# Convolution taps as diagonal products on TensorE, and products straight from PSUM, in a gated delta mixer

## The chip, the cores and the metric

The kernel runs on one core of a Trainium2 chip. The metric is the device time of one execution in microseconds; what is compared is the median of several runs. The core has five engines with a queue each: TensorE (PE) multiplies, VectorE (DVE) and ScalarE (ACT) work elementwise, GpSimd (POOL) too, and SyncE (SP) issues the transfers. All work is ordered by semaphores that the program sets.

## The reference, cut to what matters

Two transformer blocks follow each other; the second has four parts: a mixer "ab", an MLP, a mixer "c" and another MLP. The mixer "ab" projects 272 tokens (16 of them meta tokens) by one weight, and one half of it is a bidirectional gated delta rule with 4 heads of 128 channels. What concerns this case of it:

```python
def centred_conv(x, w):                      # k = 5 taps
    y = xp[:, 0:n] * w[0]
    for j in range(1, k):
        y = y + xp[:, j:j + n] * w[j]
    return y

def gated_delta_chunked(q, k, v, beta, g):   # one direction
    kb = k * beta[..., None]
    a_mat = jnp.where(strict, jnp.einsum('bhnid,bhnjd->bhnij', kb, k) * decay, 0.0)
    rhs = jnp.concatenate([v * beta[..., None], kb * jnp.exp(gc)[..., None]], axis=-1)
    sol = lax.linalg.triangular_solve(a_mat, rhs, left_side=True, lower=True, unit_diagonal=True)
    ...
    def step(s, xs):
        v_new = u_n - jnp.einsum('bhck,bhkv->bhcv', w_n, s)
        o = jnp.einsum('bhck,bhkv->bhcv', q_n, s) + jnp.einsum('bhij,bhjv->bhiv', qk_n, v_new)
        s = s * gl_n[..., None, None] + jnp.einsum('bhck,bhcv->bhkv', k_n, v_new)
        return s, o

def delta_mixer(hq, hk, hv, hz, hb, ha, conv_w, a_log, dt_bias, o_gain):
    qkv = jax.nn.silu(centred_conv(jnp.concatenate([hq, hk, hv], axis=-1), conv_w))
    ...
    fwd = gated_delta_chunked(q, k, v, beta[:, :, 0], g[:, :, 0])
    bwd = rev(gated_delta_chunked(rev(q), rev(k), rev(v), rev(beta[:, :, 1]), rev(g[:, :, 1])))
```

So v is a projection, then a convolution with five taps per channel, then silu; and its rows are multiplied by a step size beta per token and head, another one for each direction.

## The kernel before

The 272 tokens lie in the free dimension, channels in the partitions: a block of v is 128 channels x 272 tokens, and v has four, numbered 8 to 11 among the blocks of the projection. Chunks are three pieces of tokens, t = 0 (16 rows) and t = 1, 2 (128 rows); the forward direction goes through them as 0, 1, 2 and the backward one as 2, 1, 0.

The work of `delta` is written as Python generators which yield after each small step, and whose steps are put into one program order: `spread(gen, fill, share)` runs, after each step of `gen`, so many steps of `fill`. The main line is `side` (norms and decay matrices) and then `levels`, which inverts the triangular matrices for both directions: `blocks` inverts blocks of 32 x 32 in four levels, each with two `product`s (L1700) and, on VectorE, a subtraction (L1714) and a transpose (L1716), and `pairs` joins them to blocks of 128 in four steps (products L1739, L1746 and L1749, L1756, L1761). After it `scan` runs three steps for both directions in turn: L1830 multiplies the inverse by v times beta, L1842 gives the new state, L1857 the output. The fill is `filling`: first the late projection blocks 19, 20 and 12 to 15 (`rest`), then the windowed attention of the other half of the mixer (products L1545 and L1568, softmax on L1511 to L1516), and after each of its steps 1.4 steps (`VS`) of `values`. This `values` makes v: `rest` projects the blocks 8 to 11 (each is three fp32r products, high and low parts, L272 to L274, for each of 8 pieces of the inner dimension, issued in groups of six) and convolves each in `conv_late`; `silu_exp` follows (Exp, minimum on L241, Ln and Exp, and a GpSimd product on L1359); then `turned` turns v's channels into rows by transposes on TensorE (L297) and copies them out of PSUM on ScalarE (L1622). In the rows and the order, `xp` goes by the name `dec`, the helper lines L241 and L245 stand for every scale and multiply-add, and L267 for the split of a weight into high and low part. What `values` has left when the levels end runs ahead of the scan.

In `conv_late` VectorE multiplies the projected block by the norm's scale (L1366), puts it into a padded tile `xp`, and applies the five taps: one scale (`ts`, L241) and four multiply-adds (`stt`, L245). In the scan `pmul` (L1594) multiplies v's turned rows by beta on GpSimd into a tile `vb`, once for each direction and piece, and the same function makes `kdn`, k times a decay, from which L1842 makes the state.

`self.slot(hold="delta")` takes one of a few 1 MB places of SBUF for the length of the mixer; `self.ring` brings a block of weights into the next free one, and the transfer is issued on SyncE. PSUM tiles come from two rotating sets, `bank` and `aux`. `bank` is a full PSUM bank for the products, `aux` one for small steps.

Of the kernel before, what the change touches and what calls it, by code (L numbers as in the profile page):

```python
# [25 lines left out]
N2 = S + 16  # L26
# [154 lines left out]
class Kern:  # L181
# [1178 lines left out]

    def conv_late(self, p, b, rs, wc, y):
        nc = self.nc
        xp = p.tile([128, 512], F32, name="dec", bufs=3)
        nc.gpsimd.memset(xp[:, 0:2], 0.0)
        nc.gpsimd.memset(xp[:, N2 + 2:N2 + 4], 0.0)
        nc.vector.tensor_mul(xp[:, 2:N2 + 2], b, rs)  # L1366
        self.ts(y, xp[:, 0:N2], wc[:, 0:1])
        for j in range(1, 5):
            self.stt(y, xp[:, j:j + N2], wc[:, j:j + 1], y, OP.mult, OP.add)

    def ab_inproj(self, c1, p1, px, full, steps):
# [63 lines left out]
        self.exp_set(last)  # L1435

        def rest(pw, some, bank=self.bank):
            for i in some:
                b = bank()[:, :N2]
                hi, lo = self.wsplit(blk(i), nc.gpsimd if i in WP else None)  # L1440
                for k in range(8):
                    c = slice(k * 128, (k + 1) * 128)
                    self.mm3(b, (hi[:, c], lo[:, c]), (u[0][:, k], u[1][:, k]), k == 0, k == 7)
                    if k % 2 and k < 7:
                        yield
                if i >= 12:
                    nc.vector.tensor_mul(z[:, i - 12] if i < 16 else qw[:, i - 16], b, rs)
                else:
                    self.conv_late(pw, b, rs, cw[:, i], v[:, i - 8])
                yield  # L1450
# [125 lines left out]
    def delta(self, c1, p1, pw, qk, v, z, qw, vba, rest, norms, qw_norms):  # L1576
        nc, a = self.nc, self.a
        mm = nc.tensor.matmul
        def new(tag, bufs, n=128):
            if n < 128:  # L1580
                return pw.tile([128, 4 * n], F32, name=tag + "s", bufs=2)
            return pw.tile([128, 512], F32, name=tag, bufs=bufs)
# [10 lines left out]
        def pmul(out, x, y_):  # L1593
            nc.gpsimd.tensor_mul(out, x, y_)  # L1594
# [5 lines left out]

        two = [self.slot(hold="delta") for _ in range(2)]
        kn, vn = (t[:, :1536].rearrange("p (t c) -> p t c", t=3) for t in two)

        tc_ = [t[:, 1536:1824] for t in two]
        slot = self.slot(hold="delta")
        ac, uc = ([slot[:, i * 576 + d * 288:i * 576 + (d + 1) * 288] for d in range(2)] for i in range(2))

# [4 lines left out]
        for d in range(2):  # L1612
            nc.gpsimd.memset(ac[d][:, 256:288], 0.0)

        def turned(dst, x):
# [162 lines left out]
        def values():  # L1778
            yield from rest(pw, [8, 9, 10, 11])
            for h in range(4):  # L1780
                self.silu_exp(pw, v[:, h], v[:, h])
                yield
            yield from turned(vn, v)

# [22 lines left out]
        def scan(step, d):  # L1807
# [7 lines left out]
            s0 = st[d]  # L1815
            vb = new("dec", 3)
            pmul(v4(vb)[:n], v4(vn[:, t])[:n], bc(beta[:n, t, hs], n, 128))
            if step:
# [9 lines left out]
            for h in range(4):  # L1828
                o = slice(h * 128, (h + 1) * 128)
                mm(b[:n, o], u[h], vb[:n, o], start=True, stop=step == 0)  # L1830
                if step:
                    mm(b[:n, o], wT[:, h * n:(h + 1) * n], st[d][:, o], start=False, stop=True)
# [404 lines left out]
def layouts(inp):  # L2237
# [68 lines left out]
    fa = np.concatenate([fa, np.zeros((128, 3 * 1024), np.float32)], 1)  # L2306
    o["w_ab"] = ca(fa.reshape(128, 6, 4096).transpose(1, 0, 2))
    o["w_vba"] = ca(form_b(wab[:, np.concatenate([2704 + r(128), 2048 + r(16)])]))
    prm["conv_w"] = f["conv_w_a_2"][0].T.reshape(12, 128, 5).transpose(1, 0, 2).reshape(128, 60)
# [53 lines left out]
```

## Time and profile before

| | us |
|---|---|
| median of 3 runs (lowest, highest) | 1550.58 (1544.03, 1555.73) |
| the profiled execution | 1552.06 |
| its span on the core | 1550.3 |
| TensorE busy | 1480.6 (96%) |
| VectorE busy | 820.3 (53%) |
| ScalarE busy | 638.5 (41%) |
| GpSimd busy | 175.9 (11%) |

The profiled execution's mean granted TensorE clock is 0.971 of full speed; the two levels seen are 1.2 GHz (0.5) and 2.4 GHz (1.0), and a value between is a mean of both over a stretch. Times in the rows further down are counted from the start of the span. The mixer's late projections, inverse and scan lie between about 905 and 1050 us. Engine work overlaps, so a busy share is no price: what counts is which wait ends last.

### The profile page before, as it was taken

To read this page: it belongs to the slowest core of one execution; us is meant where nothing else is said; L and a number is where in the kernel's file an instruction comes from. 1 tells how busy PE (TensorE), PEld (TensorE's weight loads), DVE (VectorE), ACT (ScalarE), POOL (GpSimd) and SP (SyncE) were. 2 spreads that over 40 slices of the span, in tenths; PEclk is the share of its full clock that TensorE was granted. 3 is DMA by queue.
4 is the path that set the end of the run, shared out by engine and by line. 5 is a ranking of instruction groups with operands and counts; after the bars stand their busy time and mean duration, and the time that the engine had idled before them with its cause. 6 is when DMAs were issued, how large, how long until landed. Compare 5 with 4: busy or idle time off the path is not lost.

```text
span 1550.3 us, 26421 instructions
## 1 busy us (share of the span) xinstructions
PE 1480.6 (96%) x10806; PEld 1130.8 (73%) x10806; DVE 820.3 (53%) x1594; ACT 638.5 (41%) x1265; POOL 175.9 (11%) x226
## 2 busy tenths in 40 slices
PE   8999999989899999999998888899999999999999
PEld 7788744344388875434338877679999997899998
DVE  6686712212436782222128586557556666666665
ACT  5475411111246642111127664455444455554443
POOL 0130000000001000000005440302001123121000
PEclk9999999999999999999999898799999999999999
DMA  9345799999833579999953300036555542255530
GB/s 377 128 136 213 303 402 421 386 421 422 351 147 110 209 307 378 421 377 422 422 233 121 120 29 4 26 125 231 180 174 171 185 144 92 82 197 182 181 138 29
DMA packets 50033, 348.76 MB, mean 225 GB/s; under 512 B 5616, under 2 KB 6896, under 8 KB 8688
## 3 DMA queue, kind: packets, MB, share of 16 engines
q1 hardware_dynamic: 49904, 346.97, 58.2%
q8 instruction: 89, 1.46, 0.4%
q14 instruction: 40, 0.33, 0.1%
HBM read 345.90 MB, written 1.05 MB: 224 GB/s over the span
## 4 chain that ended last, share of the span: by engine, by line
PE 43%; DVE 4%; POOL 3%; ACT 2%; issue 2%; POOLq 0%; ACTq 0%; DVEq 0%
PE bank L274 10%; PE bank L272 10%; PE bank L273 10%; PE bank L1060 3%; PE bank L1101 2%; POOL cy L1346 1%; PE aux L297 1%; PE aux L2072 1%; ACT ring L236 1%; PE aux L1568 1%; DVE ring L267 1%; PE bank L1700 1%; PE aux L2050 1%; PE bank L1857 1%; PE aux L1545 0%
## 5 line engine op out<-in xcount | busy, mean ns | idle before, releaser
L236 ACT ACTIVATE ring<-ring 128x1024 fp32r<-128x1024 f32 (+3 forms) x189 | 186.9, 999 | 202.2 <-PE bank L274 180.2
L267 DVE TENSOR_TENSOR ring<-ring,ring 128x1024 fp32r<-128x1024 f32 x145 | 179.3, 1236 | 88.5 <-ACT ring L236 88.5
L272 PE MATMUL bank<-uh,ring 128*128 128x272 f32 (+1 forms) x744 | 219.3, 295 | 0.0
L274 PE MATMUL bank<-uh,ring 128*128 128x272 f32 (+1 forms) x744 | 215.6, 290 | 0.0
L273 PE MATMUL bank<-ul,ring 128*128 128x272 f32 (+1 forms) x744 | 214.5, 288 | 0.0
L272 PEld LDWEIGHTS bank<-uh,ring 128*128 128x128 f32 x744 | 141.7, 190 | 3.3 <-issue 2.2
L274 PEld LDWEIGHTS bank<-uh,ring 128*128 128x128 f32 x744 | 141.7, 190 | 0.8 <-DVE ring L267 0.4
L273 PEld LDWEIGHTS bank<-ul,ring 128*128 128x128 f32 x744 | 141.6, 190 | 0.7
L274 PE MATMUL bank<-rh,ring 128*128 128x272 f32 (+1 forms) x496 | 141.6, 286 | 0.0
L272 PE MATMUL bank<-rh,ring 128*128 128x272 f32 (+1 forms) x496 | 141.5, 285 | 0.0
L273 PE MATMUL bank<-rl,ring 128*128 128x272 f32 (+1 forms) x496 | 140.9, 284 | 0.0
L1073 DVE TENSOR_TENSOR hid<-hid,bank 128x512 f32<-128x512 f32 x16 | 11.0, 687 | 193.3 <-PE bank L1060 193.3
L273 PEld LDWEIGHTS bank<-rl,ring 128*128 128x128 f32 x496 | 93.8, 189 | 0.0
L272 PEld LDWEIGHTS bank<-rh,ring 128*128 128x128 f32 x496 | 93.2, 188 | 0.0
L274 PEld LDWEIGHTS bank<-rh,ring 128*128 128x128 f32 x496 | 93.0, 187 | 0.0
L245 DVE SCALAR_TENSOR_TENSOR big<-bank,gs,big 128x512 fp32r<-128x512 f32 x32 | 24.0, 751 | 99.3 <-ACT big L236 97.8
L1309 POOL TENSOR_TENSOR fr<-fr 128x272 f32<-128x272 f32 (+1 forms) x64 | 40.1, 627 | 287.7 <-DVE fr L245 283.8
L236 ACT ACTIVATE big<-bank,gs 128x512 fp32r<-128x512 f32 x32 | 22.0, 687 | 98.4 <-PE bank L1101 98.2
L1279 DVE TENSOR_TENSOR h<-h,bank 128x272 f32<-128x272 f32 (+1 forms) x80 | 33.2, 426 | 50.8 <-PE bank L274 50.8
L236 ACT ACTIVATE hid<-bank 128x512 f32<-128x512 f32 x24 | 14.3, 597 | 108.9 <-PE bank L1060 103.9
L1083 ACT COPY hidT<-bank 128x512 f32<-128x512 f32 x16 | 9.4, 586 | 118.3 <-PE bank L297 118.3
L1101 PE MATMUL bank<-big,hidT 128*64 128x512 f32 x208 | 47.8, 595 | 0.1
(677 smaller groups left out, 3434.3 us busy)
## 6 DMA issues: line engine op xcount, KB each, us to landing
ring<-w_ff SPq DMA_DIRECT2D x58, 1024.0 KB, 4.8
big<-w_gate SPq DMA_DIRECT2D x30, 1024.0 KB, 17.7
big<-w_up SPq DMA_DIRECT2D x29, 1024.0 KB, 18.0
big<-w_down SPq DMA_DIRECT2D x26, 1024.0 KB, 17.6
ring<-w_gate SPq DMA_DIRECT2D x24, 1024.0 KB, 14.2
ring<-w_down SPq DMA_DIRECT2D x24, 1024.0 KB, 17.5
ring<-w_up SPq DMA_DIRECT2D x20, 1024.0 KB, 18.6
big<-w_in SPq DMA_DIRECT2D x9, 1024.0 KB, 11.2
```

The costliest lines, as they stand in the source:

```text
L236: return self.nc.scalar.activation(out, in_, func, **kw)
L245: return (eng or self.nc.vector).scalar_tensor_tensor(out, in0, s, in1, op0=op0, op1=op1, **kw)
L267: (eng or self.nc.vector).tensor_sub(l, src, h.bitcast(F32))
L272: mm(out, lhs[0], rhs[0], start=first, stop=False)
L273: mm(out, lhs[0], rhs[1], start=False, stop=False)
L274: mm(out, lhs[1], rhs[0], start=False, stop=last)
L297: self.nc.tensor.transpose(out, in_, self.ident[:k, :k])
L1060: mm(b[e * 64:e * 64 + CAP], xg[:, k, e * CAP:(e + 1) * CAP], w[:, (2 * k + e) * 512:(2 * k + e + 1) * 512], start=k == 0, stop=k == 7)
L1101: mm(yb[n][e * 64:e * 64 + CAP], hT[:, k, e * 64:e * 64 + CAP], w[:, o:o + 512], start=k == 0, stop=k == 3)
L1279: self.nc.vector.tensor_add(self.h2[:, k, lo:], self.h2[:, k, lo:], b[:, :n])
L1309: nc.gpsimd.tensor_mul(r, r, r)
L1346: nc.gpsimd.tensor_add(y, y, t)
```

## The change

`conv_late` becomes a generator. After the multiplication into `xp` it yields, and four of the five taps are then products on TensorE that add up in one `aux` tile: each has a 128 x 128 diagonal matrix of the tap's weights as one operand and a shifted view of `xp` as the other. The fifth tap and the sum are one multiply-add on VectorE. The sixteen diagonal matrices (four blocks, four taps) come as a new input `w_dg` of 1 MB, loaded into a slot held for the mixer when `rest` first runs.

`turned` is no longer used for v. In `turned_v` the transposes of a piece go to a PSUM tile, and VectorE multiplies that tile by beta for both directions into `VB`; the forward direction at t = 0 has its four heads in one tile, the backward one has three there and the fourth in `last`. In the scan `vb` is taken from `VB`, and the GpSimd product is gone. The pieces come in the order 0, 2, 1. `VB` needs places, so the slots that weight blocks and other tiles get are others than before.

```diff
-    def conv_late(self, p, b, rs, wc, y):
+    def conv_late(self, p, b, rs, wc, y, turns):
         nc.vector.tensor_mul(xp[:, 2:N2 + 2], b, rs)
-        self.ts(y, xp[:, 0:N2], wc[:, 0:1])
-        for j in range(1, 5):
-            self.stt(y, xp[:, j:j + N2], wc[:, j:j + 1], y, OP.mult, OP.add)
+        yield
+        cb = self.aux()[:, :N2]
+        for i, j in enumerate((0, 1, 3, 4)):
+            nc.tensor.matmul(cb, turns[:, i * 128:(i + 1) * 128], xp[:, j:j + N2], start=i == 0, stop=i == 3)
+        self.stt(y, xp[:, 2:2 + N2], wc[:, 2:3], cb, OP.mult, OP.add)
...
         def rest(pw, some, bank=self.bank):
+            if not diag:
+                diag.append(self.slot(hold="delta"))
+                nc.sync.dma_start(diag[0], a["w_dg"])
...
-                    self.conv_late(pw, b, rs, cw[:, i], v[:, i - 8])
+                    yield from self.conv_late(pw, b, rs, cw[:, i], v[:, i - 8], diag[0][:, (i - 8) * 512:(i - 7) * 512])
...
-        two = [self.slot(hold="delta") for _ in range(2)]
-        kn, vn = (t[:, :1536].rearrange("p (t c) -> p t c", t=3) for t in two)
+        one, two = (self.slot(hold="delta") for _ in range(2))
+        kn = one[:, :1536].rearrange("p (t c) -> p t c", t=3)
...
+        VB = {(d, t): two[:, (2 * d + t - 1) * 512:(2 * d + t) * 512] for d in range(2) for t in (1, 2)}
+        VB[0, 0], VB[1, 0] = slot[:, 1440:1952], pw.tile([16, 384], F32, name="vb0", bufs=1)
+        last = one[:, 1824:1952]
...
+        def turned_v():
+            for t in (0, 2, 1):
+                cc = self.hcols(t)
+                n = cc.stop - cc.start
+                b = self.bank()
+                for h in range(4):
+                    self.transpose(b[:n, h * 128:(h + 1) * 128], v[:, h, cc])
+                for d in range(2):
+                    m = 4 if d == 0 or t else 3
+                    nc.vector.tensor_mul(VB[d, t][:n].rearrange("p (h c) -> p h c", h=m), v4(b)[:n, :m],
+                                         beta[:n, t, 4 * d:4 * d + m, None].to_broadcast([n, m, 128]))
+                    if m == 3:
+                        self.ts(last[:n], b[:n, 384:512], beta[:n, t, 7:8])
+                yield
...
-            yield from turned(vn, v)
+            yield from turned_v()
...
-            vb = new("dec", 3)
-            pmul(v4(vb)[:n], v4(vn[:, t])[:n], bc(beta[:n, t, hs], n, 128))
+            vb = VB[d, t]
+            vh = [last if d and t == 0 and h == 3 else vb[:, h * 128:(h + 1) * 128] for h in range(4)]
...
-                mm(b[:n, o], u[h], vb[:n, o], start=True, stop=step == 0)
+                mm(b[:n, o], u[h], vh[h][:n], start=True, stop=step == 0)
...
+    for i in range(4):
+        for k, j in enumerate((0, 1, 3, 4)):
+            dg[r(128), i, k, r(128)] = f["conv_w_a_2"][0][j, 1024 + i * 128:1152 + i * 128]
+    o["w_dg"] = dg.reshape(128, 2048)
```

How this stands in the queues is shown at three places. First TensorE, at the first product of the second level, where `ring,am` is the last piece of that level's first product, L297 with `ws` are transposes of the window's softmax and L272 to L274 are a block of the projection (six to a step, of which the first and the last are shown). Before:

```order
L1700 MATMUL bank<-ring_6932,am 32x32 x35
L272 MATMUL bank<-uh,ring_7771 128x272
L273 MATMUL bank<-ul,ring_7771 128x272
...
L274 MATMUL bank<-uh,ring_7771 128x272
L297 MATMUL aux<-prm,ws 16x128
L297 MATMUL aux<-prm,ws 128x128 x2
L272 MATMUL bank<-uh,ring_7771 128x272
...
L274 MATMUL bank<-uh,ring_7771 128x272
L1700 MATMUL bank<-qk,ring_6933 32x32 x72
```

and with the change, with its lines moved by 26:

```order
L1726 MATMUL bank<-ring_6933,am 32x32 x32
L1371 MATMUL aux<-dec,two_6952 128x272 x4
L297 MATMUL aux<-prm,ws 16x128
L297 MATMUL aux<-prm,ws 128x128 x2
L272 MATMUL bank<-uh,ring_7782 128x272
...
L274 MATMUL bank<-uh,ring_7782 128x272
L1726 MATMUL bank<-qk,ring_6933 32x32 x72
```

Block 8's four products (L1371) stand there in front of one group of six, where two groups stood.

The second place is TensorE in the pairs, from the first product (L1739, now L1765) to the last (L1761, now L1787). Before:

```order
L274 MATMUL bank<-uh,ring_8240 128x272
L1739 MATMUL bank<-wsp_6931,ring_6938 32x32 x16
L1739 MATMUL bank<-ring_6932,ring_6942 32x32 x16
...
L272 MATMUL bank<-uh,ring_8240 128x272
...
L1568 MATMUL aux<-PTw,vba 64x128 x6
L1746 MATMUL bank<-qk,ring_6938 32x32 x8
...
L297 MATMUL aux<-prm,ws 128x128 x2
L1756 MATMUL bank<-T,ring_6938 64x64 x8
L1756 MATMUL bank<-T,ring_6942 64x64 x8
L1568 MATMUL aux<-PTw,vba 64x128 x6
...
L1761 MATMUL bank<-ring_6938,qk 64x64 x8
L1761 MATMUL bank<-ring_6942,qk 64x64 x8
```

with the change:

```order
L1765 MATMUL bank<-ring_6933,ring_6943 32x32 x10
L1371 MATMUL aux<-dec,two_6952 128x272 x4
L1765 MATMUL bank<-ring_6933,ring_6943 32x32 x6
...
L272 MATMUL bank<-uh,ring_8394 128x272
...
L1576 MATMUL aux<-PTw,vba 64x128 x6
...
L1775 MATMUL bank<-ring_6943,qk 32x32 x16
L272 MATMUL bank<-uh,ring_8394 128x272
...
L1782 MATMUL bank<-T,ring_6943 64x64 x8
L272 MATMUL bank<-uh,ring_8394 128x272
...
L1576 MATMUL aux<-PTm,vba 64x16 x6
L1371 MATMUL aux<-dec,two_6952 128x272 x4
L1787 MATMUL bank<-ring_6939,qk 64x64 x8
```

Block 10's four products stand inside the first product, block 11's ahead of the last one; and block 11's projection products (two groups of six behind L1775, one behind L1782) stand where before the last of them (the row above L1739 is the end of the last group) were done.

The third place is GpSimd, from v's silu (L1359 with `v`) through the scan, `T` and `am` being `kdn`. Before:

```order
L1359 TENSOR_TENSOR v<-v,dsq 128x272 x2
L1594 TENSOR_TENSOR T<-wsp_6931,dt_6918 128x512 x3
L1359 TENSOR_TENSOR v<-v,dsq 128x272 x2
L1594 TENSOR_TENSOR dec<-ring_6932,dt_6893 16x512
L1594 TENSOR_TENSOR dec<-ring_6932,dt_6893 128x512 x3
L1359 TENSOR_TENSOR z<-z,dsq 128x272
L1594 TENSOR_TENSOR dec<-ring_6932,dt_6893 128x512
L1594 TENSOR_TENSOR am<-wsp_6931,dt_6918 16x512
L1359 TENSOR_TENSOR z<-z,dsq 128x272 x3
L1594 TENSOR_TENSOR dec<-ring_6932,dt_6893 16x512
```

with the change:

```order
L1359 TENSOR_TENSOR v<-v,dsq 128x272 x3
L1602 TENSOR_TENSOR T<-wsp_6931,dt_6918 128x512 x3
L1359 TENSOR_TENSOR v<-v,dsq 128x272
L1359 TENSOR_TENSOR z<-z,dsq 128x272
L1602 TENSOR_TENSOR am<-wsp_6931,dt_6918 16x512
L1359 TENSOR_TENSOR z<-z,dsq 128x272 x3
```

The six products into `dec` (L1594, one direction and piece each) have gone from between v's and z's; `am` is now behind one product of z.

## Rows read from the trace of the kernel before

**Rows 1.** The page: busy time by engine, and GB/s in 40 slices.
```profile
PE 1480.6 (96%) x10806; PEld 1130.8 (73%) x10806; DVE 820.3 (53%) x1594; ACT 638.5 (41%) x1265; POOL 175.9 (11%) x226
...
GB/s 377 128 136 213 303 402 421 386 421 422 351 147 110 209 307 378 421 377 422 422 233 121 120 29 4 26 125 231 180 174 171 185 144 92 82 197 182 181 138 29
```

**Rows 2.** Busy times by stretch, 920 to 1025; columns in the first row.
```profile
core 0: us, PE busy (x) PEld busy (x) DVE busy (x) ACT busy (x) POOL busy (x), PEclk, DMA share, GB/s
...
920.00:960.00 40.00, 33.37 (x1269) 27.15 (x1268) 25.70 (x78) 16.52 (x53) 6.35 (x10) 0.81 0.02 4
960.00:972.00 12.00, 12.00 (x285) 10.58 (x285) 11.46 (x31) 7.51 (x22) 3.70 (x3) 1.00 0.02 5
972.00:980.00 8.00, 4.29 (x24) 2.27 (x24) 7.17 (x16) 5.55 (x16) 4.40 (x5) 0.76 0.00 0
980.00:1000.00 20.00, 18.06 (x97) 14.59 (x96) 9.85 (x24) 9.89 (x30) 6.41 (x8) 0.58 0.00 1
1000.00:1025.00 25.00, 23.93 (x203) 20.31 (x201) 11.97 (x32) 10.64 (x29) 1.03 (x1) 1.00 0.55 191
```

**Rows 3.** Chain of waits, 965 to 987: start us, us, what.
```profile
965.92 0.44 DVE dec L1366
...
971.38 0.41 DVE v L245
...
974.34 0.77 POOL v L1359
...
975.56 1.48 ACT ring L1622 x3
...
984.84 1.04 POOL dec L1594
985.88 1.06 POOL am L1594
...
986.98 4.08 PE bank L1842 x16
```

**Rows 4.** TensorE's waits, 905 to 1050: in total, times, longest us.
```profile
PE bank L1830 <- POOL dec L1594: 2.5, 1, 2.5
...
PE bank L1842 <- POOL am L1594: 1.6, 1, 1.6
```

**Rows 5.** Chain of waits, 878 to 888, fp32 products (L1407) and one projection product.
```profile
878.71 1.81 PE aux L1407 x4
...
887.20 0.46 PE aux L1407 x2
887.66 0.12 PE bank L272
```

**Rows 6.** VectorE by line and form: duration ns min/median/max, first and last start.
```profile
L1676 DVE TENSOR_TENSOR ring<-aux,dec x4: 669/678/691, 895.4 to 909.1; 128x512 f32<-128x512 f32 x4
...
L1820 DVE TENSOR_TENSOR ring<-wsp,dt x3: 679/680/684, 971.7 to 976.4; 128x512 f32<-128x512 f32 x3
L1820 DVE TENSOR_TENSOR am<-wsp,dt x1: 670/670/670, 1013.4 to 1013.4; 16x512 f32<-16x512 f32 x1
...
L241 DVE TENSOR_SCALAR v<-dec,wsp x4: 340/358/361, 913.1 to 966.6; 128x272 f32<-128x272 f32 x4
...
L245 DVE SCALAR_TENSOR_TENSOR v<-dec,wsp,v x16: 480/496/979, 914.2 to 971.3; 128x272 f32<-128x272 f32 x16
```

**Rows 7.** Timeline of TensorE, 961 to 979: start, us, what [idle before].
```profile
961.25 0.60 PE L1739 MATMUL bank<-wsp,ring 32*32 32x32 f32 x26
...
970.04 1.90 PE L1761 MATMUL bank<-ring,qk 64*64 64x64 f32 x32
...
978.20 1.88 PE L1830 MATMUL bank<-dec,us 16*16 16x128 f32 x8 [2.51 <-POOL dec L1594]
```

**Rows 8.** Chain of waits, later: a product and a late split.
```profile
1004.49 1.83 PE bank L1842 x16
...
1040.48 1.15 DVE ring L267
```

More of the change, by code (lines that the diff above doesn't have):

```diff
@@ L1435, in ab_inproj @@
         self.exp_set(last)
+        diag = []
         def rest(pw, some, bank=self.bank):
+            if not diag:
+                diag.append(self.slot(hold="delta"))
+                nc.sync.dma_start(diag[0], a["w_dg"])
             for i in some:
@@ L1599, in delta @@
         beta, gc, gl, ec, kd, kb = self.gates(c1, p1, vba)
-        two = [self.slot(hold="delta") for _ in range(2)]
-        kn, vn = (t[:, :1536].rearrange("p (t c) -> p t c", t=3) for t in two)
-        tc_ = [t[:, 1536:1824] for t in two]
+        one, two = (self.slot(hold="delta") for _ in range(2))
+        kn = one[:, :1536].rearrange("p (t c) -> p t c", t=3)
         slot = self.slot(hold="delta")
+        tc_ = [one[:, 1536:1824], slot[:, 1152:1440]]
+        VB = {(d, t): two[:, (2 * d + t - 1) * 512:(2 * d + t) * 512] for d in range(2) for t in (1, 2)}
+        VB[0, 0], VB[1, 0] = slot[:, 1440:1952], pw.tile([16, 384], F32, name="vb0", bufs=1)
+        last = one[:, 1824:1952]
         ac, uc = ([slot[:, i * 576 + d * 288:i * 576 + (d + 1) * 288] for d in range(2)] for i in range(2))
@@ L2307, in layouts @@
     o["w_ab"] = ca(fa.reshape(128, 6, 4096).transpose(1, 0, 2))
+    dg = np.zeros((128, 4, 4, 128), np.float32)
+    for i in range(4):
+        for k, j in enumerate((0, 1, 3, 4)):
+            dg[r(128), i, k, r(128)] = f["conv_w_a_2"][0][j, 1024 + i * 128:1152 + i * 128]
+    o["w_dg"] = dg.reshape(128, 2048)
     o["w_vba"] = ca(form_b(wab[:, np.concatenate([2704 + r(128), 2048 + r(16)])]))
```

## The prediction, made before the changed kernel ran

> **What bounds the kernel now.** I read the page's busy shares first: TensorE is busy 96% of the span [rows 1]. The change lies in the delta mixer of the second block, so I then took the busy times by stretch [rows 2]. TensorE has little cover to spare there, in three different ways. From 960 to 972 us it is busy 12.00 of 12 us at a granted clock of 1.00 (the 2.4 GHz level), with VectorE busy 11.46: there the pairs of the triangular inverse are solved and v's last block is convolved. From 972 to 980 it is busy 4.29 of 8 us at a mean clock of 0.76. From 980 to 1000 it is busy 18.06 of 20 us, but at 0.58, close to the 1.2 GHz level. So one place is full, the next is starved, and the third is full of slow work. Over the 105 us of those rows TensorE is idle for 13; what is added to it has to find those holes.
>
> The chain of waits says what starves it [rows 3]. Block 11 of v is convolved on VectorE from 965.92 to 971.79, silu's last GpSimd product starts at 974.34, three ScalarE copies bring the turned rows out of PSUM (1.48 us), and later, in the scan, a GpSimd product of v by the step sizes (1.04 us) stands in front of another GpSimd product (1.06 us) for which TensorE waits until 986.98. TensorE's own waits agree: 2.5 us for the first of these products, 1.6 us for the one queued behind it [rows 4].
>
> **Part 1, the convolutions.** Four blocks lose one scale and three of four multiply-adds each on VectorE, 0.36 + 3 x 0.50 = 1.9 us at the median of the multiply-adds [rows 6], 7.4 us in all. Sixteen fp32 products of 128 x 128 by 272 columns come to TensorE. That shape is in the trace under another line [rows 5]. The row marked x2 is one product, since each fp32 product leaves two records: 0.46 us at the full clock. The row marked x4 is two at the half clock, 0.91 each. Sixteen cost 7.4 us at the full clock and 14.5 at the half. So what VectorE saves is what TensorE pays, and TensorE is the busier engine.
>
> *Blocks 8 and 9* meet the levels of the inverse. Block 8's four products stand behind the first product of the second level, where six projection products stood (0.12 to 0.13 us each at the full clock [rows 5]); block 9's stand behind a second product, and again six projection products fewer stand there. From 920 to 960 TensorE is idle 6.6 of 40 us [rows 2], because in each level it waits for VectorE's subtraction and transposes, and only a product that falls into such a wait is free. Bounds: 0 (all eight inside the idle time) and +5 (none hidden, half of them at the half clock: 4 x 0.46 + 4 x 0.91 = 5.5, less the projection products that give way). I take +1.2, nearer to the lower end: the idle time is as long as the eight products, and VectorE has 1.9 us less per block to do ahead of its transposes.
>
> *Blocks 10 and 11* meet the pairs. Before, the first product of the pairs starts at 961.25, the last at 970.04 with 1.90 us [rows 7], so the stage takes 10.7 us and TensorE is never idle in it. In the order, block 10's four products now stand inside the pairs' first product and block 11's ahead of the last: 8 x 0.46 = +3.7 us on the path. The extra step that a convolution now takes also shifts the order: 18 projection products of block 11 leave the place ahead of the pairs and stand behind their second and third products, 18 x 0.125 = +2.3 us. Where they stood they partly filled the levels' waits, so of their leaving I count only the six right before the pairs as given back, -0.8.
>
> *From the last pair to the scan* 6.3 us pass now (971.94 to 978.20 [rows 7]). The copies on ScalarE and a GpSimd product leave this stretch, 1.48 + 1.04 [rows 3], and one VectorE product out of PSUM enters it. Against that, block 11's silu starts later relative to TensorE, and VectorE's queue holds two 64-row scalings of the pairs and a softmax step in front of silu's minimum. Between 4.5 us (only the legs count) and 8.5 (only the queue counts) I take 6.5, +0.2.
>
> **Part 2, v's rows.** Gone are three ScalarE copies, 1.48 us together, and six GpSimd products of about 1.04, 6.2 us [rows 3]. VectorE gets six multiplications from PSUM into SBUF and one scale of 16 rows. Nearest rows: a product of a PSUM tile by an SBUF tile, 128 x 512, 0.68 us; one from SBUF alone, 0.68; one from SBUF with 16 rows, 0.67 [rows 6]. So 6 x 0.68 + 0.3 = 4.4 us. Only the first of these stands in front of the scan, and it is in the 6.5 above; VectorE is busy 9.85 of 20 us from 980 to 1000 [rows 2], which hides the others. By the Trainium skill (VectorE: DVE Perf Modes, Rules for kernel authors) elementwise work on a matmul's output should either take PSUM's slower reading or copy first "if you'll do many ops", which speaks against two products per tile straight from PSUM. The rows just named show no such price at this width, so the rule would add a copy of some 0.5 us per tile and save nothing.
>
> In the scan GpSimd then has nothing in front of the product for which TensorE waited: -1.6 [rows 4]. If another chain is late there instead, this is 0.
>
> **Part 3, what follows.** By the same shift one pair of window heads comes ahead of the scan, into the stretch from 972 to 980 where TensorE idles, instead of into the scan: about 2.5 us of work less at the slow clock, -2.5, or 0 if the start waits for it. Toward the end of the mixer a late split [rows 8] now comes early, but two splits for the next stage stand between the last norms on VectorE: +1, between -1 and +3 (a split is 1.15 us).
>
> **Part 4, the diagonals.** 1 MB more passes SyncE's queue, ahead of the last four weight blocks: at the 422 GB/s of the fullest slices [rows 1], 2.5 us of transfer. The DMA engines are at 2% from 920 to 972 [rows 2]. What is queued behind it are the weight blocks, which are split and multiplied only after other blocks. So 0, and at most +2.5 if one of them is needed just as it lands.
>
> **The sum.** Up to the scan: 1.2 + 3.7 + 2.3 - 0.8 + 0.2 = +6.6. Scan: -1.6 - 2.5. Tail +1, diagonals 0. Together **+2.5**. The bounds, from the low and the high end of every term, are -3 and +16; not all high ends can come at once, for the idle time that one leaves takes up another's, so I use +12. The profiled execution took 1552.06 us (span 1550.3), 1.5 above the median 1550.58, and the result is a median: 1550.6 + 2.5 = **1553**.
>
> **Rivals.** *The clock stays up.* In the stretch from 972 to 980 TensorE is half idle, and the clock after it is low [rows 2]; sixteen records of one product of the scan cost 4.08 us there and 1.83 later [rows 3, 8]. With more TensorE work up to 978 and shorter legs, the low clock could start later or not at all. The 18 us of work from 980 to 1000 would shrink by up to 9; of that the scan's own chains let about two thirds through, -6 to -9 beside the sum: 1546. For it: two legs leave the idle stretch. Against it: silu's chain of five dependent steps stays. The Trainium skill (TensorE: Matmul & The Clock Gate, Part 1) holds that the slow clock is the default and activity lifts it; by that rule this rival gains, and the rows from 960 to 1000 agree as far as they go.
>
> *The products are free.* If the 13 us of idle time take all that is added, the legs alone count: -1.5 - 1.0 - 1.6 = -4, 1546.5. Against it: the pairs' 12.00 of 12.
>
> *The slow clock spreads over the scan.* This one ends slower. If v's last block comes later than everything else, its products closing the pairs and its multiply-add standing behind other work on VectorE, TensorE idles ahead of the scan for longer than the 2.51 us of now [rows 7], and the low clock reaches past 1000: the 23.93 us of work from 1000 to 1025 [rows 2] would take up to twice as long. At 0.5 for half of it, +12, with the 6.6 of the later start +18: 1569. It decides once the way from the last pair to the scan exceeds the 8.5 us of the upper bound above.
>
> **How the numbers follow.** The sum as forecast (1550 to 1559): 0.55. The clock stays up: 0.17. The products free: 0.16. The slow clock spreads: 0.08. The rest, 0.04, to either side. The range leaves 2 in 10 out at most: from 1542 (the clock rival with its -9 and 0.3% for the runs' scatter, of which 1544 is the lowest) to 1563 (the sum with +12). About 1%, 15.5 us, is what a measurement of this kernel can tell from no change. To be faster by that needs both gains and more, 0.05; slower needs the third rival, 0.07; between them 0.88.
>
> **What would show it.** The four products of a block at 0.46 us each in the pairs and up to 0.91 in the levels; the last pair 6 to 7 us later; no wait of TensorE for GpSimd at the scan's first product or at the state's; the clock by stretch from 975 to 1025. The prediction is wrong if the scan starts less than 3 or more than 10 us later, or if the low clock after it ends elsewhere than at 1000 plus that shift.

## The result, and the profile after

The changed kernel takes 1562.1 us (median of 14 runs, 1554.3 to 1568.7) against 1549.2 us before (14 runs): a ratio of 1.0077, with a 95% interval of 1.0057 to 1.0096, so it is some 12 us slower. The sign and the range of the prediction hold, the range by less than 1 us at its upper end of 1563; its +2.5 is too small by almost 10.

The busy times of the changed kernel by stretch, with the columns of [rows 2]:

```profile
core 0: us, PE busy (x) PEld busy (x) DVE busy (x) ACT busy (x) POOL busy (x), PEclk, DMA share, GB/s
920.00:960.00 40.00, 34.36 (x1188) 27.90 (x1178) 19.98 (x72) 16.19 (x54) 4.88 (x8) 0.78 0.09 30
960.00:972.00 12.00, 11.91 (x215) 9.77 (x214) 7.55 (x20) 6.61 (x18) 0.76 (x1) 0.86 0.01 3
972.00:980.00 8.00, 7.45 (x95) 6.19 (x94) 6.31 (x7) 3.43 (x7) 4.44 (x3) 1.00 0.01 3
980.00:1000.00 20.00, 16.46 (x97) 11.17 (x96) 13.69 (x42) 10.25 (x35) 4.41 (x5) 0.74 0.00 1
1000.00:1025.00 25.00, 23.93 (x184) 19.04 (x183) 8.97 (x29) 9.46 (x28) 0.76 (x1) 0.89 0.37 125
```

Against [rows 2], VectorE is busy 7.55 us where it was busy 11.46, from 960 to 972. Part of that is relief and part is work that comes later, for from 980 to 1000 it is busy 13.69 where it was 9.85. And TensorE's clock from 960 to 972 is 0.86 instead of 1.00, the starved stretch has moved behind 980, and the slow clock with it. The 0.89 from 1000 to 1025, where it was 1.00, isn't the end of that slow stretch but a second one, as steps of 5 us show:

```profile
985.00:990.00 5.00, 4.16 (x18) 2.04 (x18) 3.88 (x14) 3.72 (x14) 2.48 (x3) 0.52 0.00 0
990.00:995.00 5.00, 4.69 (x23) 3.30 (x23) 2.92 (x9) 1.50 (x4) 0.00 (x0) 0.50 0.02 3
995.00:1000.00 5.00, 5.00 (x37) 4.06 (x35) 2.45 (x5) 2.90 (x10) 1.93 (x2) 0.95 0.00 0
...
1020.00:1025.00 5.00, 5.00 (x21) 1.91 (x19) 0.00 (x0) 0.59 (x1) 0.00 (x0) 0.50 0.59 203
```

From 1000 to 1015 the clock is 1.00; the second slow stretch lasts, with a faster part between 1030 and 1035 (0.80), until 1045.

The timeline of TensorE shows the four groups of diagonal products (two records each), the last product of the pairs and the scan's first (start, us, what, idle before):

```profile
929.46 4.00 PE L1371 MATMUL aux<-dec,two 128*128 128x272 f32 x8
...
947.87 2.10 PE L1371 MATMUL aux<-dec,two 128*128 128x272 f32 x8
...
961.73 3.58 PE L1371 MATMUL aux<-dec,two 128*128 128x272 f32 x8
...
976.48 2.07 PE L1371 MATMUL aux<-dec,two 128*128 128x272 f32 x8 [0.55 <-DVE dec L1367]
978.48 1.90 PE L1787 MATMUL bank<-ring,qk 64*64 64x64 f32 x32
...
988.32 1.88 PE L1856 MATMUL bank<-ring,us 16*16 16x128 f32 x8 [0.73 <-DVE ring L1635]
```

Against [rows 7], the last product of the pairs starts 8.4 us later and the scan 10.1 us later. Two groups ran mostly at the half clock (about 0.9 to 1.0 us a product), two mostly at the full one (about 0.5): 11.75 us in all, between the 7.4 and 14.5 of the prediction.

To compare stages between executions, I count from the first start of the decay matrices' products (L1664 before, L1690 after), for the stages ahead of it, which the change doesn't touch, scatter by some 7 us (that start lies between 885.1 and 892.1 in the profiles below). The stages end with the first starts of the levels' products, of the pairs' first, with the last start of the pairs' last, with the first starts of the scan's L1830 and of the last norms (L1871), and with the next part's first GpSimd sum (L1255). In us, worked out from first and last starts by line:

```
             to levels  levels  pairs  gap   scan  tail  rest    all
before            27.9    41.3   10.4   6.5  51.7  22.8  497.6  658.2
after             27.5    44.3   19.8   8.1  51.0  22.4  497.1  670.2
```

The 12.0 us of the two profiles agree with the 12.9 of the medians. The pairs take 9.4 us more, the levels 3.0, the gap between the last pair and the scan 1.6, and the scan gives back only 0.7. Counted from the common start, the scan begins 13.6 us later.

The chain of waits of the changed kernel through the pairs (start us, us, what):

```profile
961.15 0.64 PE bank L1765 x20
961.80 3.51 PE aux L1371 x8
965.31 0.31 PE bank L1765 x12
...
973.02 1.46 DVE ring L1846 x2
...
975.89 0.45 DVE dec L1367
...
976.48 2.07 PE aux L1371 x8
978.55 1.84 PE bank L1787 x32
...
980.41 0.69 DVE ring L241
...
981.92 0.69 DVE wst L1519 x2
...
985.96 0.78 POOL v L1359
...
989.50 0.60 DVE ring L1635
```

Block 10's products split the pairs' first product in two; block 11's wait for a multiplication on VectorE (L1367) that is queued behind three products of the scan (L1846, which run from 972.27 to 975.85); the last pair waits for block 11's products; and behind the pairs VectorE's queue holds scalings and softmax steps (L241, L245, L1519) in front of silu. TensorE's waits from 905 to 1070 name the same (in total, times, longest):

```profile
PE aux L297 <- DVE wst L1523: 2.4, 1, 2.4
...
PE bank L1856 <- DVE ring L1635: 0.7, 1, 0.7
PE aux L1371 <- DVE dec L1367: 0.6, 1, 0.6
```

GpSimd, which held TensorE up for 2.5 and 1.6 us at the scan [rows 4], is not among the waits behind the pairs any more; a softmax step and VectorE's own product out of PSUM are.

### The profile page after: what moved, and what is told of

Its sections match the earlier page's. It is cut to its first block, busy times and chain, and to the rows that moved or that the text cites. A ratio compares the mean times of both kernels' runs of the same rounds, so it can differ in the third digit from the quotient of the medians.

```text
span 1558.8 us, 26465 instructions
## 1 busy us (share of the span) xinstructions
PE 1491.8 (96%) x10838; PEld 1138.4 (73%) x10838; DVE 812.2 (52%) x1585; ACT 636.7 (41%) x1262; POOL 171.5 (11%) x220
## 4 chain that ended last, share of the span: by engine, by line
PE 46%; DVE 3%; POOL 2%; ACT 2%; issue 1%; POOLq 0%; ACTq 0%; DVEq 0%
PE bank L274 10%; PE bank L272 10%; PE bank L273 10%; PE bank L1060 3%; PE bank L1101 2%; PE aux L297 1%; POOL cy L1346 1%; PE bank L1726 1%; PE aux L1576 1%; PE aux L2098 1%; PE aux L1371 1%; PE aux L2076 1%; ACT ring L236 1%; PE bank L1856 0%; PE aux L1553 0%
## 5 line engine op out<-in xcount | busy, mean ns | idle before, releaser
L236 ACT ACTIVATE ring<-ring 128x1024 fp32r<-128x1024 f32 (+4 forms) x192 | 190.0, 1000 | 205.5 <-PE bank L274 183.5
L267 DVE TENSOR_TENSOR ring<-ring,ring 128x1024 fp32r<-128x1024 f32 x148 | 182.9, 1236 | 88.9 <-ACT ring L236 88.7
L272 PE MATMUL bank<-uh,ring 128*128 128x272 f32 (+1 forms) x744 | 218.4, 294 | 0.0
L274 PE MATMUL bank<-uh,ring 128*128 128x272 f32 (+1 forms) x744 | 214.2, 288 | 0.1
L272 PEld LDWEIGHTS bank<-uh,ring 128*128 128x128 f32 x744 | 141.3, 190 | 1.2 <-issue 0.4
L274 PE MATMUL bank<-rh,ring 128*128 128x272 f32 (+1 forms) x496 | 141.6, 286 | 0.0
L272 PE MATMUL bank<-rh,ring 128*128 128x272 f32 (+1 forms) x496 | 141.4, 285 | 0.0
L274 PEld LDWEIGHTS bank<-uh,ring 128*128 128x128 f32 x744 | 141.0, 190 | 0.6 <-DVE ring L267 0.3
L272 PEld LDWEIGHTS bank<-rh,ring 128*128 128x128 f32 x496 | 93.2, 188 | 0.0
L274 PEld LDWEIGHTS bank<-rh,ring 128*128 128x128 f32 x496 | 93.0, 187 | 0.0
L245 DVE SCALAR_TENSOR_TENSOR big<-bank,gs,big 128x512 fp32r<-128x512 f32 x32 | 24.0, 751 | 99.3 <-ACT big L236 97.8
```

The costliest lines, as they stand in the source:

```text
L236: return self.nc.scalar.activation(out, in_, func, **kw)
L245: return (eng or self.nc.vector).scalar_tensor_tensor(out, in0, s, in1, op0=op0, op1=op1, **kw)
L267: (eng or self.nc.vector).tensor_sub(l, src, h.bitcast(F32))
L272: mm(out, lhs[0], rhs[0], start=first, stop=False)
L274: mm(out, lhs[1], rhs[0], start=False, stop=last)
```

## The experiments

The theory after the result was the one of the prediction, that TensorE pays for sixteen products on its path. The rivals were that v's rows on VectorE are the cost, and that the order, shifted by the step that a convolution now takes, is. All runs were timed against the kernel before; one part in a thousand is 1.55 us. The ratios' intervals are some 2 to 3 parts to either side, so a difference between two of these kernels is known to about 3 parts, some 5 us.

**Each half alone** (rows_only, taps_only). The first kernel keeps the old convolution, and so doesn't load the diagonals:

```diff
-            yield from self.conv_late(pw, b, rs, cw[:, i], v[:, i - 8], diag[0][...])
+            self.conv_late(pw, b, rs, cw[:, i], v[:, i - 8])     # the kernel before's, five taps on VectorE
```

> The kernel before with only the second half of the change: v's rows times the step sizes straight from PSUM on VectorE, the convolution as before. The changed kernel lost 12.9 us against before (1562.1 against 1549.2). Theory P (TensorE pays for the sixteen diagonal products): this half costs nothing and may give back a little, -4 to +1 us against before, so 1545 to 1550. Rival V (VectorE's products between the last pair and the scan, and the slots moved for them, are the cost): +3 to +6 us.

Measured: 0.9978 (0.9955 to 1.0000), 1542.5 us against 1548.2: a gain of 3.4 us by the ratio, with an interval that just reaches no change. Rival V is out. Its windows over the pairs, the gap and the two halves of the scan:

```profile
957.20:967.90 10.70, 10.70 (x275) 9.40 (x274) 10.27 (x26) 6.25 (x19) 3.43 (x3) 1.00 0.02 4
967.90:972.20 4.30, 2.42 (x18) 1.30 (x18) 4.21 (x12) 2.80 (x10) 2.50 (x3) 1.00 0.00 0
972.20:997.20 25.00, 24.07 (x182) 20.57 (x183) 15.08 (x43) 12.35 (x38) 3.04 (x4) 0.86 0.12 43
997.20:1018.80 21.60, 20.53 (x156) 15.37 (x155) 10.21 (x29) 11.00 (x32) 0.00 (x0) 0.93 0.55 196
```

The gap is 4.5 us instead of 6.5, TensorE idles 1.9 us in it, and its clock stays at 1.00 through it; the scan takes 46.6 us instead of 51.7, at a clock of 0.90 over the whole of it instead of 0.80. Here the prediction's first rival, the clock that stays up, came true in part, in the half of the change that has no added products.

The second kernel has the diagonal products, and v's rows as before:

```diff
-            vb = VB[d, t]
+            vb = new("dec", 3)
+            pmul(v4(vb)[:n], v4(vn[:, t])[:n], bc(beta[:n, t, hs], n, 128))     # turned(vn, v) as before
```

> The kernel before with only the first half of the change: four taps as diagonal products, v's rows by ScalarE copies and GpSimd products as before. Theory P: nearly all of the loss is here, +11 to +17 us against before. Rival V: +7 to +10 us. If the two halves help each other, more than the whole.

Measured: 1.0113 (1.0084 to 1.0142), some 17 us. The loss is all in this half. The two halves together would make 1.0091, the whole is 1.0077, the same within the intervals.

**Without the step** (no_yield). The products follow the multiplication in the same step:

```diff
         nc.vector.tensor_mul(xp[:, 2:N2 + 2], b, rs)
-        yield
+        yield from ()
         cb = self.aux()[:, :N2]
```

> The changed kernel without the extra step between VectorE's multiplication into the padded tile and the four products, so that the later steps of v's chain and the projection products stay nearer to their old places. Rival Y (the shifted order, 18 projection products moved into the pairs, is a large part of the loss): 4 us or more faster than the changed kernel. Theory P: within 2 us of it, for the same products stay on TensorE, or slower, since TensorE now waits for the multiplication (0.44 us) at each of four places.

Measured: 1.0022 (1.0000 to 1.0043). By the ratios that is 8.5 us faster than the changed kernel, with the same sixteen products, although TensorE now waits for VectorE's multiplication. Theory P, which allowed 2 us, falls; what the step does is worth about half of the 9.9 parts that the convolutions lose (1.0077 against 0.9978). The other 4.4 parts, 6.8 us against the kernel with the rows alone, are left with the products.

**One product instead of four** (one_tap). Three of the five taps are left out:

```diff
-        for i, j in enumerate((0, 1, 3, 4)):
-            nc.tensor.matmul(cb, turns[...], xp[:, j:j + N2], start=i == 0, stop=i == 3)
+        for i, j in enumerate((0,)):
+            nc.tensor.matmul(cb, turns[...], xp[:, j:j + N2], start=True, stop=True)
```

> The changed kernel with one diagonal product per block where there are four: three of the five taps are left out of the convolution. Twelve products less, 5.5 us at the full clock and 11 at the half. Theory P: 6 to 10 us faster than the changed kernel, because all products lie on the path and most at the half clock. Rival Y: at most 3 us faster, since the order stays.

Measured: 1.0073 (1.0045 to 1.0101), like the changed kernel. Twelve products less move the end by under 1 us by the ratios (give or take 5; 3.3 us by the two profiles), where Theory P wanted 6 to 10. The chain shows where they went:

```profile
974.48 1.46 DVE ring L1846 x2
...
977.35 0.45 DVE dec L1367
...
977.93 0.70 PE aux L1371 x2
978.63 1.84 PE bank L1787 x32
```

With fewer products TensorE comes to the same place, waits there for the same multiplication behind the same three products, and the gap that follows is 8.2 us, against 8.1 in the changed kernel.

**The step without any product** (shift_only). The five taps stay on VectorE, and a step is put between the multiplication and them, in the kernel with the rows alone:

```diff
         nc.vector.tensor_mul(xp[:, 2:N2 + 2], b, rs)
+        yield
         self.ts(y, xp[:, 0:N2], wc[:, 0:1])
```

> The kernel with only v's rows straight from PSUM (0.9978 of before), and one more step in the convolution: all five taps stay on VectorE, but a step lies between the multiplication into the padded tile and the taps, as in the changed kernel. No product of a diagonal is in it. Theory Y (the later order of v's chain is itself what costs, some 9 us of the changed kernel's loss): 5 to 9 us slower than the kernel with the rows alone, 1.001 to 1.004 of before. Rival J (the step costs only together with the products, which it puts into places where TensorE or VectorE holds them up): within 2 us of the kernel with the rows alone, 0.997 to 0.999 of before.

Measured: 1.0072 (1.0045 to 1.0099), that is 9.4 parts in a thousand or 14.6 us slower than the same kernel without the step, give or take 5 us. This is more than Theory Y asked for: one added yield, and nothing else, costs as much as the whole change. The chain of this kernel behind the pairs' third product:

```profile
968.85 1.28 DVE ring L1841
...
970.15 0.44 DVE dec L1367
...
974.23 0.50 DVE v L245
...
978.99 0.77 POOL v L1359
...
982.91 0.60 DVE ring L1630
...
983.55 1.90 PE bank L1851 x8
```

and its gap and the first 25 us of its scan:

```profile
972.90:983.50 10.60, 4.81 (x26) 2.82 (x26) 8.68 (x29) 6.75 (x22) 2.50 (x5) 0.79 0.00 0
983.50:1008.50 25.00, 24.90 (x141) 20.60 (x142) 8.55 (x24) 8.54 (x26) 2.43 (x3) 0.61 0.00 1
```

Block 11's multiplication starts at 970.15, behind a product for the scan, its taps run past the last pair, silu's last product starts at 978.99, and TensorE idles 5.8 us in the gap. The scan then runs at 0.61 where the kernel without the step has 0.86. So the later place of v's chain costs in the pairs and the gap, and, as far as the slow clock follows from the longer gap, a second time in the scan.

**The pace** (vs_18). The changed kernel with v's chain at 1.8 instead of 1.4 steps to a step of the window, which makes up for the four added steps:

```diff
-VS = 1.4
+VS = 1.8
```

> The changed kernel with the pace of v's chain raised from 1.4 to 1.8 steps for each step of the window, so that the four added steps are made up for: block 11's projection ends ahead of the pairs' third product, as without the step. All sixteen products stay, and none waits for VectorE in its own step. Theory Y: as fast as the kernel without the step or faster, 0.999 to 1.003 of before. If the place of the products in the order doesn't matter (their number does): 1.006 to 1.009, like the changed kernel.

Measured: 0.9981 (0.9964 to 0.9999), 1544.4 us. The same sixteen products, the same yield, and the loss is gone, with a little more than that. Its pairs, gap and the first 25 us of the scan:

```profile
961.40:974.80 13.40, 13.40 (x271) 11.54 (x270) 11.39 (x25) 8.96 (x25) 6.02 (x4) 1.00 0.01 3
974.80:979.30 4.50, 4.42 (x45) 2.98 (x44) 3.04 (x7) 2.84 (x9) 2.53 (x4) 1.00 0.00 0
979.30:1004.30 25.00, 24.50 (x199) 21.87 (x197) 13.90 (x40) 12.64 (x38) 2.26 (x3) 0.93 0.19 53
```

TensorE idles 0.1 us in the gap and runs at 0.93 in the first 25 us of the scan. Block 11's multiplication on VectorE is now ahead of the three products of the scan, the first of which starts at 968.67, and block 11's products wait for nothing:

```profile
966.97 0.44 DVE L1367 TENSOR_TENSOR dec<-bank,nrs 128x272 f32<-128x272 f32 x1
```

**The load alone** (load_only). The kernel before with the 1 MB loaded and unused:

```diff
         def rest(pw, some, bank=self.bank):
+            if not diag:
+                diag.append(self.slot(hold="delta"))
+                nc.sync.dma_start(diag[0], a["w_dg"])
```

> The kernel before with the 1 MB of diagonals loaded into a held slot and never used. By the prediction's fourth part this is free: 0.9985 to 1.0015 of before. Rival L (the load delays the last weight blocks, or the changed slots do): +2 us or more, 1.0015 or above.

Measured: 1.0002 (0.9982 to 1.0022). The load and the slots it shifts are free within 2 parts in a thousand.

**Two blocks of four** (two_taps). Without the step, blocks 8 and 9 as products and 10 and 11 on VectorE:

```diff
+        if not on_pe:                                  # on_pe = i < 10
+            self.ts(y, xp[:, 0:N2], wc[:, 0:1])
+            for j in range(1, 5):
+                self.stt(y, xp[:, j:j + N2], wc[:, j:j + 1], y, OP.mult, OP.add)
+            return
```

> The changed kernel without the step, and with diagonal products for the blocks 8 and 9 alone; the blocks 10 and 11 are convolved on VectorE as before. With the rows alone it was 0.9978 of before, with all four blocks as products 1.0022, so the sixteen products cost some 7 us there. If the levels' idle time hides the products of 8 and 9, as I took for half of them: 0.998 to 0.9995. If all products cost alike: 1.000. If those of the levels cost more (slow clock): 1.001 to 1.002.

Measured: 0.9980 (0.9957 to 1.0003), the same as with the rows alone. So the products of blocks 10 and 11, in the pairs, cost the difference to 1.0022, some 6.5 us, give or take 5. The intervals are too wide to say whether the levels' products are hidden or cost a few us; by the profile the levels take 43.7 us against 40.4.

**The pace without products** (rows_vs18, before_vs18). The same edit in two kernels without diagonals:

```diff
-VS = 1.4
+VS = 1.8     # in the kernel with the rows alone, and in the kernel before
```

> The kernel with only v's rows straight from PSUM (0.9978 of before) and v's chain at a pace of 1.8 instead of 1.4. If the changed kernel at 1.8 (0.9981) is fast because v is ready early and the scan then runs short, and its products cost nothing: 0.997 to 0.999 here too. If its products still cost some 5 us, which the pace hides: 0.993 to 0.996. If the pace only makes up for the added step, and VectorE's five taps crowd the pairs when they come earlier: 0.998 to 1.001.

> The kernel before with the pace of 1.8 and nothing else. Theory Y says that what counts is how late v's chain ends against the last pair; before, the gap from the last pair to the scan is 6.5 us. With v earlier the gap should shrink to 4 to 5 us and the clock in the scan rise: 0.996 to 0.999. If GpSimd's products hold the gap instead: 0.999 to 1.001.

Measured: 1.0017 (0.9994 to 1.0041) and 1.0068 (1.0043 to 1.0093). Both are slower than the same kernels at 1.4 by 6 and 10.5 us. Theory Y as written, that an earlier v is better, falls here. A step given to v is a step taken from the windowed attention, since both are drawn from the same fill: the paced kernel before has a tail of 37.7 us instead of 22.8, with the window's last heads in it (the last product L1568 starts at 1050.2 instead of 1037.6). Its pairs take 15.7 us instead of 10.4, and not because five taps a block crowd VectorE: TensorE is busy all the time, at the half clock, and VectorE for 9.75 us.

```profile
959.90:975.60 15.70, 15.70 (x249) 13.48 (x248) 9.75 (x31) 8.04 (x24) 3.83 (x4) 0.50 0.01 3
```

In rows_vs18 the pairs are partly starved instead: 13.5 us, of which TensorE is busy 10.96, at 0.86.

**A faster pace for the changed kernel** (vs_22).

```diff
-VS = 1.4
+VS = 2.2
```

> The changed kernel at a pace of 2.2. All four blocks' products stand ahead of the pairs' third product. If an earlier v helps further: 0.994 to 0.997. If 1.8 has already taken v off the end, so that other steps end last: 0.997 to 1.001, and the gap from the last pair to the scan stays at 4 to 5 us.

Measured: 1.0051 (1.0026 to 1.0076). The tail is 38.6 us. Of 1.4, 1.8 and 2.2 the middle pace is the best here: it is a balance, not a direction.

**Each product twice** (twice_vs18), in the changed kernel at 1.8:

```diff
+        for n in range(2):
             for i, j in enumerate((0, 1, 3, 4)):
                 nc.tensor.matmul(cb, turns[...], xp[:, j:j + N2], start=i == 0, stop=i == 3)
```

> The changed kernel at a pace of 1.8 with every diagonal product done twice (the sum is begun anew, so the result is the same): 16 fp32 products more, 7.4 us at the full clock and 14.5 at the half. Theory P (each product lies on TensorE's path): 6 to 12 us slower than with them once, 1.002 to 1.006 of before. Rival F (in this order the idle time of TensorE takes them): within 2 us, 0.997 to 0.9995.

Measured: 1.0020 (1.0005 to 1.0035), 3.9 parts or 6 us more than with them once, 0.38 us for each added product. This is at the lower edge of Theory P, and with some 4 us to either side it is a rough price, 0.15 to 0.6 us a product, about a full-clock row (0.46 [rows 5]). Other things moved as well: in the profile the pairs take 22.0 us instead of 13.2, TensorE is busy 20.00 of these at a clock of 0.77, and block 11's eight products take 6.37 us. That the kernel with the products at 1.8 (0.9981) beats the same pace without them (1.0017) by 5.6 us would fit a relief of VectorE that pays for them there; but rows_vs18 also lacks the four added steps, so its v comes earlier still, and no run separates the two.

The stages of the kernels that carry the argument, in us of their profiles and counted as above:

```
             levels  pairs   gap  scan  tail    all   ratio
before         41.3   10.4   6.5  51.7  22.8  658.2
load_only      42.1   11.0   6.0  55.4  21.9  661.5  1.0002
rows_only      40.4   10.5   4.5  46.6  22.6  650.0  0.9978
taps_only      47.5   19.6  12.7  49.8  22.3  676.6  1.0113
shift_only     38.0   15.9  10.8  54.3  22.0  666.2  1.0072
no_yield       43.4   16.2   5.6  52.2  21.8  663.9  1.0022
one_tap        43.1   17.6   8.2  51.0  22.3  666.9  1.0073
two_taps       43.7   11.3   4.2  46.7  22.3  652.8  0.9980
vs_18          46.5   13.2   4.7  39.5  29.9  658.3  0.9981
twice_vs18     48.4   22.0   4.7  38.3  27.5  665.5  1.0020
rows_vs18      41.7   13.5   6.8  41.2  32.3  660.9  1.0017
before_vs18    42.6   15.7   7.3  42.0  37.7  670.8  1.0068
vs_22          41.7   15.5   7.4  43.9  38.6  671.7  1.0051
after          44.3   19.8   8.1  51.0  22.4  670.2  1.0077
```

One profile is one execution; the last column is what was measured over many, and the two differ by up to 6 us. How far a single stage can scatter shows in load_only: by the ratio it is the kernel before, and its scan takes 3.7 us more. So a difference of a few us in one stage, between two profiles, is not to be read; the 5 to 10 us in the pairs are.

## Why the prediction was right in sign and short in size

*Part 2, v's rows*, was right: the legs on ScalarE and GpSimd leave TensorE's waits, and this half alone gains 3.4 us. VectorE's product out of PSUM took 0.67 to 0.68 us in the changed kernel, the price taken.

*Part 4* was right: the load alone is 1.0002.

*Blocks 8 and 9* (+1.2, with -0.8 given back): the levels with what leads to them took 2.6 us more instead of 0.4, and block 8's group of products ran at the half clock (4.00 us instead of 1.84). This is inside the bound of +5.

*Blocks 10 and 11*, +3.7 + 2.3: **here the working failed.** The pairs took 9.4 us more. I priced the products at the full clock, and block 10's ran at the half (3.58 us instead of 1.84), and I left out the wait for block 11's multiplication (0.55 us) behind the scan's three products, which stand in front of it on VectorE's queue. That makes 2.3 of the 3.4 us by which the pairs went beyond the 6.0 forecast; the rest is not assigned. But the step that really failed is the one on the order: "the extra step that a convolution now takes also shifts the order", for which I counted 2.3 us of moved products, and took 2.5 back elsewhere. The runs put the price of that step, without any product, at 14.6 us (1.0072 against 0.9978), and with the products in place at 8.5 (1.0077 against 1.0022), and that of all sixteen products at about 6 to 7. I had the sizes the wrong way round. What the step does is to move v's chain behind other work on VectorE: block 11's multiplication behind the scan's products, its silu behind scalings and softmax steps, so that TensorE reaches the end of the pairs and the gap before v is there. A faster pace, which puts the multiplication back ahead of these products, takes the loss away (0.9981). In the changed kernel VectorE's relief and the products nearly cancel (1.0072 with the step alone, 1.0077 with both), which is what the first part of the prediction had said of them and then did not carry through.

*From the last pair to the scan*: +0.2 forecast, 1.6 measured, inside the bounds: 7.9 us by the prediction's count (980.38 to 988.32), near the upper one of 8.5. The third rival was to decide beyond 8.5. Its mechanism isn't what the rows show, although its lower clock past 1000 is there (0.89 from 1000 to 1025, 1.00 before): the slow stretch that begins in the gap ends at about 995, and by the mean clock lasts 10 us, where it lasted 21 before.

*The scan*, -1.6 - 2.5: it gave back 0.7. The wait for GpSimd is gone, a head pair moved ahead and the first slow stretch is shorter, but the second one, from 1020 on, stands against these gains: with the rows alone, at clocks of 0.86 and 0.93, the scan is 5.1 us shorter. That the slow clock behind the pairs follows from the idle gap is argued from how the two go together in these profiles. From the last pair to 24 us into the scan, TensorE is at the half clock, as worked out from the mean clock of that stretch, for 0 to 7 us where the gap has 0 to 1.9 us of idle time (twice_vs18, vs_18, two_taps, rows_only), and for 17 to 24 us where it has 3.1 to 5.8 (no_yield, load_only, before, taps_only, shift_only). The changed kernel and one_tap, with 3.2 us of idle time, lie between with 10; and no run changed the idle time alone. Three kernels at a raised pace (rows_vs18, before_vs18, vs_22), whose gaps have no idle time and yet ran wholly at 0.50, with scans at 0.80 and 0.81, don't fit this, and why the clock of the changed kernel falls again at 1020 stays open: TensorE idles 1.07 us just ahead, at 1017.44, but it does so in the kernel before too, at 1014.23, and there the clock stays at 1.00 to 1025.

*The sum*: its terms make +3.5, not +2.5, for the tail's +1 was named and not added; and their low and high ends make about -2 and +18, not -3 and +16. The forecast would have been 1554, the range the same. The tail (+1 forecast, -0.4 measured) was not late.

*The chances*: within 1% had 0.88, and 0.8% was measured. But 1562.1 lies outside the 1550 to 1559 that had 0.55, and by the signs that the prediction set for itself it is wrong: the scan was not to start more than 10 us later, and starts 10.1 us later by the clock of the profiles and 13.6 counted from the common start; the low clock was to end at 1000 plus that shift, and ends at about 995 and then comes back from 1020 to 1045. That the time stayed inside the range is in part luck: the allowance of +12 was made for the high ends of other terms, and what filled it was the step, which the sum had at about nothing.

## What to carry to other kernels

In a program whose order is made by counting steps, an added yield is a change of its own: price it as a move of everything behind it, and try it without the rest of the change, and try the pace that makes up for it. Work moved from a busy VectorE to a busier TensorE can still come out even, if it lands in places where TensorE waits; the same products cost some 6.5 us in the pairs and nothing that these runs can tell from nought in the levels. Of this change the half on v's rows is worth keeping alone (0.9978), and the whole at a pace of 1.8 (0.9981) is as good; both gains are small beside their intervals.

## What the runs showed of the hardware

VectorE's products of two SBUF tiles slow down beside GpSimd's. In the changed kernel three of them (L1846) met GpSimd's three products into `T`, from 972.3 to 976.8. The first, which began 0.05 us ahead of GpSimd's first, took 0.69 us, the second 1.39 and the third 1.52, against 0.68 each before [rows 6]; GpSimd's took 1.48 instead of 1.24. The rows of VectorE (duration ns min/median/max) and GpSimd in the changed kernel:

```profile
L1846 DVE TENSOR_TENSOR ring<-wsp,dt x3: 693/1385/1523, 972.3 to 974.3; 128x512 f32<-128x512 f32 x3
```

```profile
972.32 4.44 POOL L1602 TENSOR_TENSOR T<-wsp,dt 128x512 f32<-128x512 f32 x3 [2.22 <-PE bank L1782]
```

The Trainium skill (GPSIMD Engine Reference, Key points) says that GpSimd shares its SBUF interfaces with VectorE and names contention with VectorE instructions of two SBUF inputs; these rows agree, with a factor of 2 for the two products that began while GpSimd was at work. It is one more reason why block 11's multiplication came late.

The half clock (1.2 GHz) also met a stretch in which TensorE was wholly busy with fp32 products: in the 3.6 us of block 10's group the granted clock was 0.58, behind 6.7 us in which TensorE had been busy for 1.77 of 3.00 and 2.59 of 3.70 us at a clock still near 1.00.

```profile
955.00:958.00 3.00, 1.77 (x144) 1.43 (x142) 2.46 (x11) 2.10 (x8) 0.00 (x0) 1.00 0.02 5
958.00:961.70 3.70, 2.59 (x63) 2.25 (x63) 3.52 (x13) 1.80 (x5) 0.00 (x0) 0.95 0.02 4
961.70:965.30 3.60, 3.60 (x16) 2.52 (x14) 3.43 (x9) 1.40 (x4) 0.00 (x0) 0.58 0.00 0
```

So a price at the full clock, for work that follows a partly idle stretch, can be too low; that the idle time ahead is the cause was not tried by itself, and block 11's group, right behind a wait of 0.55 us, took 2.07 us, mostly at the full clock.
